# Hybrid encoder trunk: the background row sums of the modulation one batch at a time, loaded a unit ahead, and the first value weights split in the front

## The chip, the cores and the metric

One core of one Trainium2 chip. The metric is the time of one execution in device microseconds (us), as the median of a few runs. PE is the tensor engine (matmuls), DVE the vector engine (VectorE), ACT the scalar engine, POOL GpSimd, SP the engine that issues nearly all DMAs (SyncE).

## The reference

Two batches, a prompt and a sample, of 512 rows and 1024 columns each go through one layer in float32. What matters here:

```python
c_act = jax.nn.silu(c)
mod = c_act @ w_ada[l] + b_ada[l]
sh1, sc1, g1, sh2, sc2, g2 = jnp.split(mod, 6, axis=-1)
h = rms_norm(x, norm1_g[l]) * (1.0 + sc1) + sh1
proj = h @ w_in[l]                       # 768 columns for attention, 4 x 512 for retention
o_a = windowed_attention(...)            # 8 heads, 2 of keys and values, window 128
o_r = bidirectional_retention(...)       # 4 heads, chunks of 128, forward and backward
x = x + g1 * (concat(o_a, o_r) @ w_out[l])
h = rms_norm(x, norm2_g[l]) * (1.0 + sc2) + sh2
x = x + g2 * (square(relu(h @ w_mlp1[l])) @ w_mlp2[l])
```

and a last normalisation. The modulation `mod` has six sections of 1024 numbers for each batch: section 0 is sh1, 1 is sc1, 2 is g1, 3 is sh2, 4 is sc2 and 5 is g2.

## The kernel before

**Products.** A float32 product is made of three matmuls (`mm3`, L122 to L124): each operand is split into a high part, cast by ACT (`split_high`, L93, tiles `wh_...`), and a low part, the difference, made by VectorE (L99, tiles `wl_...`). Weights that both batches need are split once, for batch 0, and both parts are stored in device memory (`kept_...`) and loaded again for batch 1 (`kept_unit`, L117).

**Stages.** The *front* normalises batch 0 and makes the first 768 columns of its projection (`first`, keys, values and queries of attention). It is a list of steps written by hand (`FRONT`), and each engine keeps the order of that list up to the step P.7.0 (`pin`). P.k.c is the part of column block c from the 128 rows k; `keep.k` stores the split weights of k. After the front work goes by *units*, each with one 512 KB weight: load, split, matmuls (`pj_rv`, `pj_rq`, ...). Phase 1 has 16 units for batch 0 (4 of the retention's values, rv, and 12 of its queries, keys and gates, rq, rk, rg). Phase 2 has 22 units for batch 1 (6 of attention, which load what the front kept, 4 rv, 12 others). Phase 3 has the 8 units of batch 0's output projection (`po`, weights `wo`). Then come batch 1's output projection and the feed-forward part, which takes from about 500 us to the end.

**Between the units.** The weight of unit n+1 is loaded while unit n is computed (`run_units`). Each unit has two halves, and behind each half `between` moves the blocks of attention (`psc` scores, `ppt`, `po`) and of retention on by a step: `prs` are the scores of retention, VectorE multiplies them with a decay table (`rsf`, L409), ACT and VectorE split them (`rsc`, L411 and L412), PE makes `py`, ACT copies it (`ryt`, L429), PE transposes it (`pyn`), VectorE takes its mean and variance (`bn`, `mv`, L437 and L438), POOL takes the power (`rrs`), ACT normalises (`ryn`, L447), PE transposes back (`pyb`). `ks` and `qs` are the split keys and queries of attention.

**The background.** What batch 1's first normalisation and the later sections of `mod` need is not made by matmuls but by sums along rows on VectorE: a 128 x 1024 tile of the transposed weights (`raw_adat_...`) times the activations of one batch, summed (L172, `jka_...`, where the product itself goes to a junk tile out of the six buffers of tag `f2`, which `ryt` and others use too). There are 60 such sums on 36 loaded tiles: 12 for batch 1 alone (sections 1 and 0), and 24 tiles of sections 2, 4 and 3 with both batches. `run_units` takes one tick of the background at the end of each unit; a tick issues the load of one tile and right behind it the sums, one or two, of that tile:

```python
    def ada_unit(sec, kc, bs, dst, name, bias=None):
        t = raw_unit(w_ada_t[sec, kc], f"adat_{name}_{sec}_{kc}", sec > 1)
        reduce_unit(t, sec, kc, bs, dst, name, bias)
```

Sections 0 and 1 load into three buffers shared with the weights (tag `raw`), the others into the 32 buffers of tag `r4`. Behind the front a scheduler sets each engine's order: the program gives priorities, and what its own model takes for ready goes first. So neighbouring sums can come to stand together, and a load can stand in SP's queue behind a load that still waits for a buffer.

Of the kernel before, what the change touches and what calls it, by code (L numbers as in the profile page):

```python
# [32 lines left out]
def trunk_kernel(ctx, tc, x0, x1, x0_t, x1_t, params, gate2_bias, w_ada_first, w_ada_t, w_ada_gate2, w_in_first, w_in,  # L33
# [62 lines left out]
    def split_unit(src, name, n):  # L96
        t = raw_unit(src, name)
        w = split_high(t, name)
        nc.vector.tensor_sub(w[1], t, f(w[0]))  # L99
# [69 lines left out]

    def reduce_unit(t, sec, kc, bs, dst, name, bias=None):  # L170
        for b in bs:
            nc.vector.tensor_tensor_reduce(junk(f"jka_{name}_{sec}_{kc}_{b}"), t, cb[:, b, :], 1.0,  # L172
                                           bcol[:, sec * KC + kc:sec * KC + kc + 1] if bias is None else bias,
                                           ALU.mult, ALU.add, dst(b))

    def mod_chunk(which, is_scale, kc, bs):
        sec = which * 3 + (1 if is_scale else 0)
        if is_scale:
            ada_unit(sec, kc, bs, lambda b: mod_a[which][:, kc, b:b + 1], "s", onep[:, which * KC + kc:which * KC + kc + 1])
            for b in bs:  # L180
                a_ = mod_a[which][:, kc, b:b + 1]
                nc.vector.tensor_tensor(a_, a_, gcol[which][:, kc:kc + 1], ALU.mult)
        else:
            ada_unit(sec, kc, bs, lambda b: mod_s[which][:, kc, b:b + 1], "s")

    def first_mods(b):

        for kc in [k for k in range(KC) if k not in BOTH]:
            for s in (1, 0):
                mod_chunk(0, s == 1, kc, (b,))  # L190
                yield

    def ada_columns(which, is_scale):
        for kc in range(KC):
            mod_chunk(which, is_scale, kc, range(NB))
            yield

    def gate_rows(which):

        gm = const.tile([P, NB, KC], F32, name=f"gm_{which}")  # L200
        for kc in range(KC):
            ada_unit(which * 3 + 2, kc, range(NB), lambda b: gm[:, b, kc:kc + 1], "g")
            yield
        pg = aux_bank(f"pgt_{which}")
        nc.tensor.transpose(pg[:NB * KC, :P], gm.rearrange("p b k -> p (b k)"), ident)
        gr_ = mwork.tile([NB * KC, P], F32, tag="st", name=f"gr_{which}", bufs=8)
        nc.scalar.copy(gr_, pg[:NB * KC, :P])
        nc.gpsimd.dma_start(gates[which * NB:(which + 1) * NB, :].rearrange("b (k n) -> (b k) n", n=P), gr_)
        yield
# [1309 lines left out]
```

## Time and profile before

| | |
|---|---|
| median of 3 runs | 1142.35 us (1141.02 to 1143.53) |
| the profiled execution | 1146.14 us, its span 1144.4 us |
| busy in the span: PE, DVE, ACT, POOL | 1095.9, 878.1, 502.3, 40.8 us |
| mean granted clock of PE | 0.986 |
| DMA: moved, mean rate | 232.73 MB, 203 GB/s |

A row of a timeline gives the start, the length, the engine, the line of the kernel, the operation with its output and inputs, and in brackets how long the engine stood idle before it and what released it. Matmul rows overlap, since PE pipelines them: 0.39 us long, they start every 0.23 us.

### The profile page before, as it was taken

The numbers are of one execution on the slowest core, as the hardware profiler recorded it, in microseconds if no ns is written. First come the engines' busy times: TensorE is split into PE (matmuls) and PEld (weight loads), VectorE is DVE, ScalarE is ACT, GpSimd is POOL, SyncE is SP. The second block draws the span as 40 slices with busy tenths as digits, with TensorE's granted clock in tenths as the row PEclk, the third lists the DMA queues.
The fourth block names the chain that finished last, engine by engine and source line by source line (L and its number), as shares of the span: only waits on it lengthen the run. The fifth ranks groups of instructions, "written<-read, shape, count | busy, mean of one in ns | idle before, by whom it ended". The sixth has DMA issues, their size and how long they took to land.

```text
span 1144.4 us, 14016 instructions
## 1 busy us (share of the span) xinstructions
PE 1095.9 (96%) x4997; PEld 893.3 (78%) x4997; DVE 878.1 (77%) x1474; ACT 502.3 (44%) x861; POOL 40.8 (4%) x54
## 2 busy tenths in 40 slices
PE   8989999999899799998999999999999999999996
PEld 5778887777688578887878888888887888888885
DVE  8879888677777656698998787877659854499685
ACT  6565766334552335345433333333344543334341
POOL 1000000000000000100000000000000000001112
PEclk9989999999999979999999999999999999999999
DMA  9976798765455738951655355534693565625503
GB/s 371 361 291 226 246 346 293 224 204 166 147 169 181 271 119 304 352 181 47 214 182 184 138 184 175 185 138 147 199 390 101 166 197 189 221 91 183 179 26 148
DMA packets 86746, 232.73 MB, mean 203 GB/s; under 512 B 8578, under 2 KB 20882, under 8 KB 86676
## 3 DMA queue, kind: packets, MB, share of 16 engines
q1 hardware_dynamic: 86228, 231.51, 58.5%
q8 instruction: 39, 0.64, 0.2%
q10 hardware_dynamic: 288, 0.31, 0.1%
q14 instruction: 31, 0.25, 0.1%
q0 software_dynamic: 160, 0.02, 0.0%
HBM read 160.75 MB, written 71.06 MB: 203 GB/s over the span
## 4 chain that ended last, share of the span: by engine, by line
PE 68%; DVE 16%; DMA 8%; ACT 3%; issue 3%; POOL 1%; SPq 1%; POOLq 0%; DVEq 0%; ACTq 0%
PE px_None L901 12%; PE x L1304 11%; PE y L1304 10%; PE py_None L901 9%; PE po L122 3%; PE po L123 2%; PE po L124 2%; DVE jka_s L172 2%; DMA raw_adat_s<-in_w_ada_t_dram 2%; DMA raw_adat_g<-in_w_ada_t_dram 2%; PE ppt L379 1%; PE po L386 1%; PE psc L353 1%; DMA ur<-spill 1%; DVE jka_f L172 1%
## 5 line engine op out<-in xcount | busy, mean ns | idle before, releaser
L1244 DVE TENSOR_TENSOR uc_l<-ur,uc_h 128x1024 fp32r<-128x1024 f32 x56 | 68.4, 1221 | 53.7 <-ACT uc_h L1244 36.6
L1304 PE MATMUL x<-wc_l,uc_h 128*128 128x512 f32 x256 | 99.8, 390 | 0.8 <-DVE wc_l L1244 0.8
L1304 PE MATMUL x<-wc_h,uc_h 128*128 128x512 f32 x256 | 99.4, 389 | 0.5 <-DVE u L919 0.5
L1304 PE MATMUL x<-wc_h,uc_l 128*128 128x512 f32 x256 | 99.6, 389 | 0.0
L1244 ACT CAST uc_h<-ur 128x1024 fp32r<-128x1024 f32 x56 | 58.8, 1051 | 74.1 <-PE x L1304 30.9
L1304 PE MATMUL y<-wc_h,uc_h 128*128 128x512 f32 x192 | 74.7, 389 | 0.0
L1304 PE MATMUL y<-wc_l,uc_h 128*128 128x512 f32 x192 | 74.7, 389 | 0.0
L1304 PE MATMUL y<-wc_h,uc_l 128*128 128x512 f32 x192 | 74.7, 389 | 0.0
L1244 ACT CAST wc_h<-w 128x1024 fp32r<-128x1024 f32 x48 | 50.4, 1050 | 48.1 <-PE x L1304 23.9
L1244 DVE TENSOR_TENSOR wc_l<-w,wc_h 128x1024 fp32r<-128x1024 f32 x48 | 58.5, 1220 | 13.6 <-ACT wc_h L1244 11.4
L1304 PEld LDWEIGHTS x<-wc_l,uc_h 128*128 128x128 f32 x256 | 48.0, 188 | 11.6 <-DVE wc_l L1244 1.6
L1304 PEld LDWEIGHTS x<-wc_h,uc_h 128*128 128x128 f32 x256 | 48.1, 188 | 10.9 <-issue 0.9
L1304 PEld LDWEIGHTS x<-wc_h,uc_l 128*128 128x128 f32 x256 | 48.1, 188 | 9.8
L122 PE MATMUL po<-wh_wo,ms 128*128 128x512 f32 x128 | 51.8, 405 | 0.0
L124 PE MATMUL po<-wh_wo,ms 128*128 128x512 f32 x128 | 50.9, 398 | 0.0
L123 PE MATMUL po<-wl_wo,ms 128*128 128x512 f32 x128 | 50.8, 397 | 0.0
L806 ACT CAST wc_s4h<-raw_w 128x1024 fp32r<-128x1024 f32 x16 | 16.8, 1052 | 62.2 <-PE px_None L901 36.6
L363 ACT ACTIVATE st<-st,negm 128x256 f32<-128x256 f32 (+1 forms) x64 | 35.2, 555 | 15.5 <-DVE negm L358 15.5
L1304 PEld LDWEIGHTS y<-wc_l,uc_h 128*128 128x128 f32 x192 | 36.0, 188 | 7.5
L1304 PEld LDWEIGHTS y<-wc_h,uc_h 128*128 128x128 f32 x192 | 36.0, 188 | 7.5
L1304 PEld LDWEIGHTS y<-wc_h,uc_l 128*128 128x128 f32 x192 | 36.0, 188 | 7.4
L411 ACT CAST rsc<-rsf 128x512 fp32r<-128x512 f32 x32 | 19.7, 621 | 49.2 <-DVE rsf L409 49.2
(375 smaller groups left out, 3026.7 us busy)
## 6 DMA issues: line engine op xcount, KB each, us to landing
ur<-spill SPq DMA_DIRECT2D x56, 512.0 KB, 4.3
raw_w<-in_w_mlp_dram SPq DMA_DIRECT2D x32, 512.0 KB, 3.5
spill<-s SPq DMA_DIRECT2D x64, 256.0 KB, 3.2
w<-in_w_mlp_dram SPq DMA_DIRECT2D x32, 512.0 KB, 4.5
raw_adat_s<-in_w_ada_t_dram SPq DMA_DIRECT2D x28, 512.0 KB, 6.2
spill<-u SPq DMA_DIRECT2D x48, 256.0 KB, 2.0
raw_ada<-in_w_ada_t_dram SPq DMA_DIRECT2D x12, 512.0 KB, 9.6
x<-in_x_dram SPq DMA_DIRECT2D x12, 512.0 KB, 8.2
```

The source lines that it names most:

```text
L122: nc.tensor.matmul(ps, lhs[0], rhs[0], start=start, stop=False)
L123: nc.tensor.matmul(ps, lhs[0], rhs[1], start=False, stop=False)
L124: nc.tensor.matmul(ps, lhs[1], rhs[0], start=False, stop=stop)
L172: nc.vector.tensor_tensor_reduce(junk(f"jka_{name}_{sec}_{kc}_{b}"), t, cb[:, b, :], 1.0, bcol[:, sec * KC + kc:sec * KC + kc + 1] if bias ...
L353: nc.tensor.matmul(psc[:, :w], qs[hh][:, isl], k_[:, s, j0 * P:j1 * P], start=(s == 0), stop=(s == 1))
L363: nc.scalar.activation(st[hh][:, :w], st[hh][:, :w], AF.Exp, bias=negm[:, hh:hh + 1], scale=0.125, accum_out=den[:, hh:hh + 1])
L379: nc.tensor.transpose(pt[:, hh * P:(hh + 1) * P], st[hh][:, jj * P:(jj + 1) * P], ident)
L411: nc.scalar.copy(sc[sb][:, 0, :], sf)
L806: nc.scalar.copy(hi, src)
L901: self.last = nc.tensor.matmul(bank[:, cs], x[:, k, :], y, start=first and k == 0 and i == 0, stop=last and k == 3 and i == 2, skip_group_ ...
L1244: last_split[:] = [nc.scalar.copy(hi, src), nc.vector.tensor_sub(lo, src, f(hi))]
L1304: nc.tensor.matmul(out, left[n][x][:, i, ts_], right[n][y][:, i, :], start=first and i == 0 and k == 0, stop=end and i == 1 and k == 2, sk ...
```

## The change

**The background.** One generator, `background_mods`, takes the place of `first_mods`, `gate_rows` and `ada_columns`. It goes through the same tiles in the same order (12 for batch 1 alone, then sections 2, 4, 3 with both batches). Each of its steps makes one sum. The load of tile n+1 is issued at the first step of tile n, and all tiles are in the 32 buffers of `r4`. Each sum is issued with `issue_after` on VectorE's last instruction before it in the program, so that the scheduler does not put it ahead of that one. The ticks are no longer taken at the end of a unit but in `between`, 0.7 for each half of a unit, so 1.4 for a unit.

**The front.** The load of the first value weights (`rvl.0`) stands behind `wi.7`, the last load of the front's own weights; their cast (`rvh.0`) and difference (`rvs.0`) ahead of P.7.0, and the load of the second ones behind these. The `keep` steps are spread among the earlier P steps.

```diff
-    def ada_unit(sec, kc, bs, dst, name, bias=None):
-
-        t = raw_unit(w_ada_t[sec, kc], f"adat_{name}_{sec}_{kc}", sec > 1)
-        reduce_unit(t, sec, kc, bs, dst, name, bias)
...
+    def last_of(engine):
+        return next(i for i in reversed(nc.cur_bb.bb.instructions) if i.engine == engine)
+
+    gm = const.tile([P, NB, KC], F32, name="gm")
+
+    def background_mods():
+        todo = [(s, kc, (1,)) for kc in range(KC) if kc not in BOTH for s in (1, 0)]
+        todo += [(s, kc, range(NB)) for s in (2, 4, 3) for kc in range(KC)]
+
+        def load(n):
+            return raw_unit(w_ada_t[todo[n][0], todo[n][1]], f"adat_{n}", True) if n < len(todo) else None
+        nxt = load(0)
+        yield
+        for n, (sec, kc, bs) in enumerate(todo):
+            t, nxt = nxt, load(n + 1)
+            which, is_scale = divmod(sec, 3)
             for b in bs:
...
+                with tc.issue_after(last_of(mybir.EngineType.DVE)):
+                    reduce_unit(t, sec, kc, (b,), lambda _: dst, "b",
+                                onep[:, which * KC + kc:which * KC + kc + 1] if is_scale == 1 else None)
+                    if is_scale == 1:
+                        nc.vector.tensor_tensor(dst, dst, gcol[which][:, kc:kc + 1], ALU.mult)
                 yield
...
+            if sec == 2 and kc == KC - 1:
+                pg = aux_bank("pgt")
...
@@ between @@
+        clock[2] += clock[3]
+        while clock[2] > 0.999:
+            clock[2] -= 1.0
+            tick_background()
         clock[1] = min(clock[1] + rate, 3.0)
...
@@ run_units @@
-    def run_units(units, rate, hooks={}, pace=1.0):
-        due = 0.0
+    def run_units(units, rate, hooks={}, pace=0.7):
+        clock[3] = pace
         nxt = units[0].load()
...
             for _ in u.use(cur):
                 between(rate)
-            due += pace
-            if due > 0.999:
-                due -= 1.0
-                tick_background()
...
@@ ret_v_units, load @@
-                return split_unit(w_in_v[kq], f"rv{b}_{kq}", 512)
+                t = one.pop(("rv", kq), None) or raw_unit(w_in_v[kq], f"rv{b}_{kq}")
+                return split_raw(t, f"rv{b}_{kq}", 512)
...
+    def step_rvs(kq):
+        t, w = one["rv", kq]
+        nc.vector.tensor_sub(w[1], t, f(w[0]))
+        first_v[kq].loaded([x.rearrange("p (a n) -> p a n", n=512) for x in w])
...
@@ FRONT, its last lines @@
-hm.7 hl.6 wl.7 P.6.0 lg.6 P.6.1 lg.7 hl.7 P.6.2 P.6.3 P.6.4 P.6.5 keep.6 P.7.0 P.7.1 P.7.2 P.7.3
-P.7.4 P.7.5 keep.7
+wl.7 P.6.0 keep.4 lg.6 P.6.1 lg.7 hl.7 P.6.2 P.6.3 keep.5 P.6.4 P.6.5 rvh.0 rvs.0 rvl.1 P.7.0 P.7.1
+P.7.2 P.7.3 keep.6 P.7.4 P.7.5 keep.7
...
-    background.extend([first_mods(1), gate_rows(0), ada_columns(1, True), ada_columns(1, False)])
+    background.append(background_mods())
```

On PE at the end of the front, before (`first` is the projection, `pvt_a` a transposition of the values, `psc` the first scores, `pj_rv` the first value unit):

```order
L124 MATMUL first_312<-h_0_7_510,wil_441 128x512
L316 MATMUL pvt_a_635<-ident,vt_a_566 128x128 x4
L353 MATMUL psc_0_0_0_648<-ks_0_553,qs_0_573 128x256 x2
L353 MATMUL psc_0_0_1_652<-ks_0_553,qs_0_573 128x256 x2
L122 MATMUL pj_rv_0_619<-wh_rv_0_606,h_0_0_243 128x512
L122 MATMUL pj_rv_1_620<-wh_rv_0_606,h_0_0_243 128x512
L353 MATMUL psc_0_0_2_656<-ks_0_553,qs_1_581 128x256 x2
L122 MATMUL pj_rv_2_621<-wh_rv_0_606,h_0_0_243 128x512
L123 MATMUL pj_rv_0_619<-wl_rv_0_607,h_0_0_243 128x512
L124 MATMUL pj_rv_0_619<-wh_rv_0_606,h_0_0_243 128x512
```

and now:

```order
L126 MATMUL first_313<-h_0_7_511,wil_446 128x512
L124 MATMUL pj_rv_0_620<-wh_rv_0_551,h_0_0_244 128x512
L125 MATMUL pj_rv_0_620<-wl_rv_0_552,h_0_0_244 128x512
L126 MATMUL pj_rv_0_620<-wh_rv_0_551,h_0_0_244 128x512
L124 MATMUL pj_rv_0_620<-wh_rv_0_551,h_0_1_261 128x512
L125 MATMUL pj_rv_0_620<-wl_rv_0_552,h_0_1_261 128x512
L126 MATMUL pj_rv_0_620<-wh_rv_0_551,h_0_1_261 128x512
L314 MATMUL pvt_a_636<-ident,vt_a_573 128x128 x4
L124 MATMUL pj_rv_1_621<-wh_rv_0_551,h_0_0_244 128x512
L125 MATMUL pj_rv_1_621<-wl_rv_0_552,h_0_0_244 128x512
L126 MATMUL pj_rv_1_621<-wh_rv_0_551,h_0_0_244 128x512
L124 MATMUL pj_rv_1_621<-wh_rv_0_551,h_0_1_261 128x512
```

Matmuls of the first value unit, 12 in these rows, moved ahead of the scores.

On SP early in phase 2, before (the `kept_first` loads are weights of attention for batch 1; `raw_adat_g_3` is the tile of section 2 whose sums are `jka_g_3_0` and `jka_g_3_1`):

```order
L88 DMA raw_adat_g_2_2023<-in_w_ada_t_dram 128x1024
L117 DMA wh_q_0_2197<-kept_first 128x8x128
L117 DMA wl_q_0_2199<-kept_first 128x8x128
L117 DMA wh_q_1_2259<-kept_first 128x8x128
L117 DMA wh_q_2_2342<-kept_first 128x8x128
L88 DMA raw_adat_g_3_2109<-in_w_ada_t_dram 128x1024
L117 DMA wl_q_1_2261<-kept_first 128x8x128
L117 DMA wl_q_2_2344<-kept_first 128x8x128
```

and now (the numbers after `raw_adat` only count tiles; 1988 is the fifth tile of section 2, 2108 the sixth, 2216 the seventh):

```order
L119 DMA wl_v_2127<-kept_first 128x8x128
L88 DMA raw_adat_1988<-in_w_ada_t_dram 128x1024
L119 DMA wl_q_0_2201<-kept_first 128x8x128
L119 DMA wh_q_0_2199<-kept_first 128x8x128
L119 DMA wh_q_1_2261<-kept_first 128x8x128
L88 DMA raw_adat_2108<-in_w_ada_t_dram 128x1024
L523 DMA kept_t_101<-dtab_3_2184 128x896
L119 DMA wh_q_2_2342<-kept_first 128x8x128
L119 DMA wl_q_1_2263<-kept_first 128x8x128
L119 DMA wh_q_3_2412<-kept_first 128x8x128
L119 DMA wl_q_2_2344<-kept_first 128x8x128
L88 DMA raw_adat_2216<-in_w_ada_t_dram 128x1024
```

The tiles stand earlier among the same weights: the one ahead of `wl_q_0` is now the fifth, where the third stood before, and the sixth stands ahead of `wh_q_2`, which the fourth stood behind.

On DVE at the end of phase 2, before (`jka_s_5` and `jka_s_6` are tiles 5 and 6 of section 3; `bn_1` is the retention's second head, `wl_wo` a weight of the output projection):

```order
L291 TENSOR_TENSOR rk_3_3798<-pj_rk_3_3768,rk_3_3798 128x512
L99 TENSOR_TENSOR wl_wo_0_1_3910<-raw_wo_0_1_3907,wh_wo_0_1_3909 128x1024
L172 ISA jka_s_5_0_3713,mod_s_90<-raw_adat_s_5_3711,cb,cols 128x1024
L172 ISA mod_s_90 128x1
L172 ISA jka_s_5_1_3715,mod_s_90<-raw_adat_s_5_3711,cb,cols 128x1024
L172 ISA mod_s_90 128x1
L172 ISA jka_s_6_0_3760,mod_s_90<-raw_adat_s_6_3758,cb,cols 128x1024
L172 ISA mod_s_90 128x1
L172 ISA jka_s_6_1_3762,mod_s_90<-raw_adat_s_6_3758,cb,cols 128x1024
L172 ISA mod_s_90 128x1
L437 BN_STATS bn_1_0_3807<-pyn_1_3801 128x6
```

and now (`jka_b_1` and `jka_b_2` are tiles 1 and 2 of section 3):

```order
L289 TENSOR_TENSOR rq_3_3725<-pj_rq_3_3697,rq_3_3725 128x512
L170 ISA jka_b_1_1_3728,mod_s_90<-raw_adat_3601,cb,cols 128x1024
L170 ISA mod_s_90 128x1
L170 ISA jka_b_2_0_3755,mod_s_90<-raw_adat_3648,cb,cols 128x1024
L170 ISA mod_s_90 128x1
L101 TENSOR_TENSOR wl_wo_0_0_3874<-raw_wo_0_0_3871,wh_wo_0_0_3873 128x1024
L435 BN_STATS bn_1_0_3783<-pyn_1_3777 128x6
L289 TENSOR_TENSOR rk_3_3774<-pj_rk_3_3740,rk_3_3774 128x512
L436 BN_AGGR mv_1_3782<-bn_1_0_3783 128x2
```

Of the four sums ahead of `bn_1` two are left, and they belong to earlier tiles; the sums of tiles 5 and 6 moved into phase 3.

More of the change, by code (lines that the diff above doesn't have):

```diff
@@ L96, in split_unit, with split_raw @@
     def split_unit(src, name, n):
-        t = raw_unit(src, name)
+        return split_raw(raw_unit(src, name), name, n)
+    def split_raw(t, name, n):
         w = split_high(t, name)
@@ L174, in reduce_unit @@
                                            ALU.mult, ALU.add, dst(b))
[L176 to L179, printed above, removed]
-            for b in bs:
[L181 to L190, printed above, removed]
-                yield
[L193 to L209, printed above, removed]
+    def last_of(engine):
+        return next(i for i in reversed(nc.cur_bb.bb.instructions) if i.engine == engine)
@@ new lines, in trunk_kernel @@
+    gm = const.tile([P, NB, KC], F32, name="gm")
[9 more added lines that the diff above has]
+            which, is_scale = divmod(sec, 3)
+            for b in bs:
+                dst = (mod_s[which], mod_a[which], None)[is_scale]
+                dst = gm[:, b, kc:kc + 1] if dst is None else dst[:, kc, b:b + 1]
+                with tc.issue_after(last_of(mybir.EngineType.DVE)):
[3 more added lines that the diff above has]
+                        nc.vector.tensor_tensor(dst, dst, gcol[which][:, kc:kc + 1], ALU.mult)
+                yield
+            if sec == 2 and kc == KC - 1:
+                pg = aux_bank("pgt")
+                nc.tensor.transpose(pg[:NB * KC, :P], gm.rearrange("p b k -> p (b k)"), ident)
+                gr_ = mwork.tile([NB * KC, P], F32, tag="st", name="gr", bufs=8)
+                nc.scalar.copy(gr_, pg[:NB * KC, :P])
+                nc.gpsimd.dma_start(gates[0:NB, :].rearrange("b (k n) -> (b k) n", n=P), gr_)
+                yield
@@ L529, in trunk_kernel @@
     background, stages, active, extra, later = [], [], [], [], []
-    clock = [0, 0.0]
+    clock = [0, 0.0, 0.0, 0.0]
     def tick_background():
@@ L581, in __init__, with loaded @@
             self.load, self.use, self.done, self.keep = load, use, done, keep
-    def run_units(units, rate, hooks={}, pace=1.0):
-        due = 0.0
+        def loaded(self, w):
+            self.load = lambda: w
+    def run_units(units, rate, hooks={}, pace=0.7):
+        clock[3] = pace
         nxt = units[0].load()
@@ L649, in trunk_kernel @@
     ret_v = [[], []]
+    one = {}
     hT_of = [[], []]
@@ L935, in store @@
                 nc.sync.dma_start(spill[g][p, :, i, :], t)
-    wi, halves, sums, mr, hm, banks, open_banks, one = {}, {}, {}, {}, {}, {}, {}, {}
+    wi, halves, sums, mr, hm, banks, open_banks = {}, {}, {}, {}, {}, {}, {}
     order = (4, 5, 0, 1, 2, 3)
@@ L1086, in step_warm, with step_rvl, step_rvh @@
             nc.tensor.transpose(b_[:, :P], ident, ident)
+    def step_rvl(kq):
+        one["rv", kq] = raw_unit(w_in_v[kq], f"rv0_{kq}")
+    def step_rvh(kq):
+        one["rv", kq] = one["rv", kq], split_high(one["rv", kq], f"rv0_{kq}")
+    def step_rvs(kq):
+        t, w = one["rv", kq]
+        nc.vector.tensor_sub(w[1], t, f(w[0]))
+        first_v[kq].loaded([x.rearrange("p (a n) -> p a n", n=512) for x in w])
     logs = log_decays()
-    steps = dict(x=step_x, nat=step_nat, tr=step_tr, wi=step_wi, tanh=step_tanh, cact=step_cact, cbt=step_cbt, cbc=step_cbc,
+    steps = dict(rvl=step_rvl, rvh=step_rvh, rvs=step_rvs, x=step_x, nat=step_nat, tr=step_tr, wi=step_wi, tanh=step_tanh, cact=step_cact, cbt=step_cbt, cbc=step_cbc,
                  sq=step_sq, ad=step_ad, ns=step_ns, nv=step_nv, nr=step_nr, rbt=step_rbt, rbc=step_rbc, xn=step_xn,
@@ L1103, in trunk_kernel @@
 P.1.5 P.2.0 tr.6.0 wl.3 P.2.1 wh.4 hl.3 P.2.2 wi.5 xn.2 P.2.3 tr.7.1 P.2.4 C.5.1 hh.4 P.2.5 hm.4
-tr.7.0 P.3.0 C.5.0 wh.5 P.3.1 wi.6 P.3.2 wl.4 hh.5 wi.7 P.3.3 hm.5 hl.4 P.3.4 C.6.1 P.3.5 wh.6 P.4.0
-C.6.0 P.4.1 wh.7 P.4.2 wl.5 P.4.3 hl.5 P.4.4 xn.3 P.4.5 keep.0 keep.1 keep.2 keep.3 keep.4 P.5.0
-lg.0 C.7.1 hh.6 P.5.1 lg.1 hm.6 P.5.2 lg.2 C.7.0 P.5.3 lg.3 wl.6 P.5.4 lg.4 hh.7 P.5.5 keep.5 lg.5
-hm.7 hl.6 wl.7 P.6.0 lg.6 P.6.1 lg.7 hl.7 P.6.2 P.6.3 P.6.4 P.6.5 keep.6 P.7.0 P.7.1 P.7.2 P.7.3
-P.7.4 P.7.5 keep.7
+tr.7.0 P.3.0 C.5.0 wh.5 P.3.1 wi.6 P.3.2 wl.4 hh.5 wi.7 rvl.0 P.3.3 hm.5 hl.4 P.3.4 C.6.1 P.3.5 wh.6
+P.4.0 keep.0 C.6.0 P.4.1 wh.7 P.4.2 wl.5 P.4.3 keep.1 hl.5 P.4.4 xn.3 P.4.5 P.5.0 keep.2 lg.0 C.7.1
+hh.6 P.5.1 lg.1 hm.6 P.5.2 lg.2 C.7.0 P.5.3 keep.3 lg.3 wl.6 P.5.4 lg.4 hh.7 P.5.5 lg.5 hm.7 hl.6
+wl.7 P.6.0 keep.4 lg.6 P.6.1 lg.7 hl.7 P.6.2 P.6.3 keep.5 P.6.4 P.6.5 rvh.0 rvs.0 rvl.1 P.7.0 P.7.1
+P.7.2 P.7.3 keep.6 P.7.4 P.7.5 keep.7
     """.split()
@@ L1112, in trunk_kernel @@
     first = attn_units(hT_of[0], 0)
+    first_v = ret_v_units(hT_of[0], 0)
     for name in FRONT:
@@ L1149, in norm_x1 @@
             yield
-    background.extend([first_mods(1), gate_rows(0), ada_columns(1, True), ada_columns(1, False)])
-    units = ret_v_units(hT[0], 0)
+    background.append(background_mods())
+    units = first_v
     for h in range(RH):
-        units += ret_units(hT[0], 0, h)
-    run_units(units, 1.3, {7: lambda: extra.append(norm_x1())}, pace=1.0)
+        units = units + ret_units(hT[0], 0, h)
+    run_units(units, 1.3, {7: lambda: extra.append(norm_x1())})
     units = attn_units(hT[1], 1) + ret_v_units(hT[1], 1)
```

## The prediction

> **What bounds the kernel now.** I read the list of engines on the page first, then the run cut into stages at places where PE's picture changes, then PE's chain of waits, then the timelines around the waits. The page says that PE is the bound:
>
> ```profile
> span 1144.4 us, 14016 instructions
> PE 1095.9 (96%) x4997; PEld 893.3 (78%) x4997; DVE 878.1 (77%) x1474; ACT 502.3 (44%) x861; POOL 40.8 (4%) x54
> ```
>
> So 1144.4 - 1095.9 = 48.5 us of PE idle is all that can be won without taking matmuls out, plus what PE loses where its clock is halved. The change takes no matmul out. The stages (columns: window, length, busy us and count for PE, PEld, DVE, ACT, POOL, then granted clock, DMA share, GB/s) say where these 48.5 us lie:
>
> ```profile
> 57.00:68.00 11.00, 6.96 (x19) 5.28 (x20) 10.57 (x19) 6.38 (x11) 0.00 (x0) 0.69 0.57 196
> 68.00:171.00 103.00, 102.98 (x506) 84.44 (x505) 86.56 (x213) 69.03 (x156) 1.99 (x1) 1.00 0.82 285
> 171.00:206.00 35.00, 33.23 (x152) 26.14 (x150) 28.93 (x57) 23.74 (x38) 2.02 (x2) 1.00 0.92 297
> 206.00:292.00 86.00, 76.15 (x341) 59.74 (x342) 62.91 (x154) 31.97 (x75) 2.73 (x3) 0.97 0.59 189
> 345.00:413.00 68.00, 58.16 (x240) 44.98 (x239) 48.47 (x97) 21.29 (x40) 2.01 (x2) 0.90 0.53 183
> 413.00:486.00 73.00, 73.00 (x347) 60.70 (x346) 44.27 (x85) 30.14 (x57) 5.02 (x6) 1.00 0.84 302
> 238.58:241.99 3.41, 1.66 (x7) 0.99 (x8) 2.83 (x10) 1.74 (x5) 1.01 (x1) 1.00 0.83 233
> 241.99:245.40 3.41, 3.41 (x10) 2.73 (x10) 3.38 (x6) 1.79 (x4) 0.00 (x0) 0.50 0.18 74
> ```
>
> Three places are at stake: the handover from the front (57 to 68: 4.0 us idle, clock 0.69), the attention and early retention of batch 1 (206 to 292: 9.9 us) and the end of batch 1's retention (345 to 413: 9.8 us, clock 0.90). Phase 1 (68 to 171) and phase 3 (413 to 486) have PE full, so there the change can only lose.
>
> **What ends these waits.** PE's own rows (start, length, what it waited for):
>
> ```profile
> 56.10 0.60 PE L316 MATMUL pvt_a<-ident,vt_a 128*128 128x128 f32 x4
> 58.92 0.50 PE L353 MATMUL psc<-ks,qs 128*128 128x256 f32 x2 [2.22 <-DVE qs L331]
> 61.54 0.77 PE L353 MATMUL psc<-ks,qs 128*128 128x256 f32 x2 [2.12 <-DVE qs L331]
> 67.61 0.53 PE L123 MATMUL pj_rv<-wl_rv,h 128*128 128x512 f32 x1
> 220.28 0.50 PE L122 MATMUL py<-rsc,rv 128*128 128x512 f32 x1 [0.86 <-ACT rsc L411]
> 228.84 0.50 PE L122 MATMUL py<-rsc,rv 128*128 128x512 f32 x1 [1.42 <-ACT rsc L411]
> 240.14 0.50 PE L122 MATMUL pj_q<-h,wh_q 128*128 128x512 f32 x1 [1.58 <-DVE qs L331]
> 289.56 0.63 PE L122 MATMUL pj_rq<-h,wh_rq 128*128 128x512 f32 x1 [2.79 <-DVE rv L291]
> 393.70 0.66 PE L433 MATMUL pyn<-ident,ryt 128*128 128x128 f32 x4 [2.97 <-ACT ryt L429]
> 399.98 1.52 PE L452 MATMUL pyb<-ident,ryn 128*128 128x128 f32 x4 [4.23 <-ACT ryn L447]
> 406.55 0.80 PE L122 MATMUL py<-rsc,rv 128*128 128x512 f32 x1 [2.09 <-ACT rsc L411]
> ```
>
> The producers named (rsc, qs, ryn) are short. What makes them late stands ahead of them on VectorE: a pair of row sums, and ahead of the pair a load that has not landed. VectorE's waits from 50 to 460 us, its timeline at two of these places, and SyncE's queue, which issued that load late:
>
> ```profile
> DVE jka_s L172 <- DMA raw_adat_s<-in_w_ada_t_dram: 12.3, 6, 4.3
> DVE jka_g L172 <- DMA raw_adat_g<-in_w_ada_t_dram: 11.4, 5, 3.5
> 199.25 10.45 SPq L117 DMA_DIRECT2D wh_q<-kept_first  x2
> 209.75 0.65 SPq L88 DMA_DIRECT2D raw_adat_g<-in_w_ada_t_dram  x1
> 214.94 1.28 DVE L172 CUSTOM_DVE_ANT_0 jka_g<-raw_adat_g,cb,cols 128x1024 bf16<-128x1024 f32 x1 [2.66 <-DMA raw_adat_g<-in_w_ada_t_dram]
> 225.04 1.29 DVE L172 CUSTOM_DVE_ANT_0 jka_g<-raw_adat_g,cb,cols 128x1024 bf16<-128x1024 f32 x1 [3.49 <-DMA raw_adat_g<-in_w_ada_t_dram]
> 391.69 1.28 DVE L172 CUSTOM_DVE_ANT_0 jka_s<-raw_adat_s,cb,cols 128x1024 bf16<-128x1024 f32 x1
> 396.51 0.29 DVE L437 BATCH_NORM_STATS2 bn<-pyn 128x6 f32<-128x128 f32 x1
> ```
>
> At 225.04 VectorE stands still for 3.49 us, then sums twice, and only then makes the rsf and rsc that PE takes at 228.84. At 391.69 nothing is late, but four sums in a row take 391.69 to 396.51 = 4.82 us (1.205 each), and the normalisation on which PE's 4.23 us wait hangs begins behind them. Together the seven waits listed from 220 on are 0.86 + 1.42 + 1.58 + 2.79 + 2.97 + 4.23 + 2.09 = 15.9 us.
>
> **The background, step by step.** The number of loads, of row sums and their reading stays. Three things change. (1) One sum per tick, so at most one or two stand together: 1.2 us ahead of a producer in place of 2.4 or 4.8. (2) The load goes out when the unit before it starts. Until now the latency stood openly in VectorE's queue, 12.3 + 11.4 = 23.7 us in 11 waits; with two ticks of lead, and a tick every 0.7 of a unit, the load has 13.4 us (phase 2 is 206 to 413 us for 22 units, 9.4 us each, with 1.4 ticks a unit, so a tick lasts 6.7 us) where SyncE's row shows 5.2 us from issue at 209.75 to use at 214.94. (3) It can still be held in SyncE's queue behind a load that waits for a buffer, as at 199.25; in the changed order the same kept loads of q stand there, one sum later, so I leave part of the first wait standing.
>
> What I take for the seven waits: 0.86 to 0.3, 1.42 to 0.5, 1.58 to 0.6, 2.79 to 0.4 (no four sums ahead of rv), 2.97 to 0 (ryt needs no buffer that a row of sums holds), 4.23 to 1.0 (a POOL power and a copy are left), 2.09 to 0.9. That leaves 3.7, and 15.9 - 3.7 = 12.2 us go. The other small waits of 200 to 412 I leave as they are.
>
> The clock comes on top. From 241.99 to 245.40 it is 0.50 after a stretch in which PE was busy 1.66 us of 3.41, though its longest wait there was 1.58 us. Each such stretch costs 3.41 / 2 = 1.7 us. The window 345 to 413 at clock 0.90 loses 0.10 * 58.16 = 5.8 us of its busy time (I count 5.3, three stretches with the wait at 406.55 taken out), and before it there are two single stretches, at 241.99 and from 289.56 on, where the first row is 0.63 and not 0.40 long: 3.4 us. Of these 8.7 us I take 5.3 as won, and leave two stretches, since waits of 0.5 to 1 us stay. The Trainium skill, "TensorE: Matmul & The Clock Gate", Part 1, in "HAM oscillation", puts the limit at idle gaps over some 3.4 us. The trace disagrees here, since 1.58 us within a half-idle stretch was enough; by the page the two stretches would also go, and the sum would be larger by 3.4 us.
>
> In phase 3 the sums come new: some 10 now stand there (46 units, 0.7 a half: 64 ticks for 62 of them), 10 * 1.2 = 12 us on a VectorE that has 73.00 - 44.27 = 28.7 us free, and 5 loads of 0.5 MB on queues at 0.84. PE never waits there now. The last sums feed the second normalisation at the phase's end, which the order puts behind them as before. I cost it at 0 with an upper bound of 5 * 0.5 MB / 302 GB/s = 8.7 us if no transfer were hidden. Phase 1 gets one or two loads more at a DMA share of 0.82 to 0.92: 0 by cover of PE's full queue, bounded by 2 * 0.5 MB / 297 GB/s = 3.5 us. For new waits from sums that may no longer be moved aside I take 1.5 us off (one sum, 1.2, once or twice exposed); the ends are 0 and 62 * 1.2 = 74, which needs every sum on PE's path and is far from rows in which PE is 96% busy.
>
> Background: 12.2 + 5.3 - 1.5 = 16.0 us.
>
> **The front, step by step.** VectorE's chain ks, qs is what PE waits for twice, while the first value weights are split only behind it:
>
> ```profile
> 51.53 2.06 SPq L88 DMA_DIRECT2D raw_rv<-in_w_in_v_dram  x2
> 60.86 1.99 ACT L93 CAST wh_rv<-raw_rv 128x1024 fp32r<-128x1024 f32 x2
> 56.76 0.69 DVE L303 TENSOR_TENSOR ks<-first,ks 64x512 fp32r<-64x512 f32 x1 [1.27 <-ACT ks L302]
> 58.19 4.54 DVE L331 TENSOR_TENSOR qs<-first,qs 64x512 fp32r<-64x512 f32 x7
> 62.75 2.36 DVE L99 TENSOR_TENSOR wl_rv<-raw_rv,wh_rv 128x1024 fp32r<-128x1024 f32 x2
> 65.05 0.63 PE L122 MATMUL pj_rv<-wh_rv,h 128*128 128x512 f32 x1
> 65.48 0.63 PE L123 MATMUL pj_rv<-wl_rv,h 128*128 128x512 f32 x1
> 229.43 0.40 PE L122 MATMUL pj_q<-h,wh_q 128*128 128x512 f32 x1
> 229.66 0.41 PE L123 MATMUL py<-rsc,rv 128*128 128x512 f32 x1
> ```
>
> Now the load goes out ahead of the 16 stores of keep, cast and difference ahead of the last step, and 18 of unit 0's 24 matmuls stand between the last of kc 7 and the fourth pair of psc. A 512-column matmul starts every 229.66 - 229.43 = 0.23 us at full clock and every 65.48 - 65.05 = 0.43 us at half. 18 * 0.23 = 4.1 us of work for the 2.22 + 2.12 = 4.3 us of wait. From 61.54 to 67.9 PE runs at half clock, which costs another 3.2 us. At stake: 7.5. Against it: the cast (1.0) and the difference (1.2) now stand ahead of the ks and qs chain. VectorE has 1.27 us idle at 56.76 that cover it if the difference falls there, else qs comes 1.2 us later. One half-clock stretch (1.7) may stay. I take 7.5 - 0.8 - 1.7 = 5.0, between 0 (the difference late, the same wait under another name) and 7.5.
>
> **Sum.** 16.0 + 5.0 = 21.0 us. The profiled execution took 1146.1 us (span 1144.4 and 1.7 around it), 3.8 above the median of 1142.35. 1146.1 - 21.0 = 1125.1 for it; against the median 1121.4, called 1122, since an execution 3.8 us quicker may have a little less idle to give.
>
> **Rivals.** A: only part comes. New producers (the power on POOL, 1.0 us a head, ACT's casts) take the places of the sums, half-clock stretches stay: the 5.0 of the front and a third of the 16: 1142.35 - 10 = 1132, between 1127 and 1140. For it: 7 of the listed waits name ACT and DVE, not the load itself. Chance 0.22.
>
> B: all goes: 15.9 + 8.7 + 7.5 = 32 us, 1110. [...] Chance 0.07.
>
> C: slower. Loads in the spare buffers wait for a buffer that PE frees, and in SyncE's queue the weights stand behind them; a sum in fixed order then holds VectorE for it. Its place is 160 to 210 us, where a weight is already late:
>
> ```profile
> 160.72 11.08 DMA raw_rq<-in_w_in_dram
> ```
>
> That load took 11.08 us, where the DMA share goes from 0.82 to 0.92. If loads ahead lengthen each of the 12 weight loads of retention by 3.5 us beyond its lead (two of these rows wait 2.7 and 3.5 on VectorE), the loss is 42 and the time 1163; it decides from 21 / 12 = 1.75 us a load on. The Trainium skill, "DMA: Bandwidth & Descriptors", "Issuing engines are not separate DMA queues", has all transfers interleave on the same 16 engines, which speaks for C: an early load takes its bandwidth from a weight. The trace agrees as far as that one load goes (11.08 us); at the share of 0.59 of 206 to 292 it shows 5.2 us. Chance 0.08.
>
> D: no change. The sums move, but the chain rsf, rsc, ryn was late for itself, and the front's wait goes to the next one: 1142, chance 0.06.
>
> The forecast has 0.57. Two runs of this kernel differ by 1143.53 - 1141.02 = 2.5 us, so 0.2% (2.3 us) is about what can be told from no change. Faster: 0.57 + 0.22 + 0.07 = 0.86, less 0.01 for A's upper edge. The likeliest case alone is 1115 to 1128; the range goes from B's 1110 to 1138, within A's upper part, and leaves C and D out.
>
> **What would show it.** Right: 57 to 68 at 9 us busy or more with pj_rv ahead of the first psc; no wait of VectorE for raw_adat over 1 us; at most two sums in a row; the windows 206 to 292 and 345 to 413 shorter by 6 and 9 us, clock 0.97 and more; phase 3 still full. Wrong: waits of PE in 68 to 206 or in phase 3, VectorE waiting for raw_adat with rsf behind it, or wl_rv ahead of qs with psc at 61 us as before.

## The result and the profile after

The changed kernel takes 1115.07 us (median of 5 runs, 1113.65 to 1116.22), the kernel before 1142.35 (1141.02 to 1143.53): 27.3 us less, a ratio of 0.976 with a 95% interval of 0.9746 to 0.9775. The forecast was 1122, with a range of 1110 to 1138. The head of the page and the stages that the prediction cut (same windows and columns):

```profile
span 1113.7 us, 14016 instructions
PE 1081.6 (97%) x4997; PEld 886.7 (80%) x4997; DVE 878.2 (79%) x1474; ACT 502.6 (45%) x861; POOL 39.4 (4%) x54
...
57.00:68.00 11.00, 9.10 (x44) 7.02 (x43) 10.02 (x22) 6.17 (x13) 0.00 (x0) 1.00 1.03 390
68.00:171.00 103.00, 99.60 (x484) 82.01 (x482) 89.48 (x215) 68.15 (x154) 1.02 (x1) 0.98 0.83 300
171.00:206.00 35.00, 33.12 (x151) 25.94 (x150) 27.95 (x56) 23.64 (x38) 2.85 (x2) 1.00 0.79 254
206.00:292.00 86.00, 85.20 (x417) 69.61 (x416) 69.88 (x181) 42.46 (x106) 2.74 (x3) 1.00 0.58 189
345.00:413.00 68.00, 66.72 (x302) 54.06 (x301) 49.39 (x98) 26.03 (x47) 3.02 (x3) 1.00 0.73 259
413.00:486.00 73.00, 71.87 (x353) 59.55 (x352) 59.52 (x109) 32.13 (x68) 3.10 (x6) 1.00 0.77 282
```

VectorE and ACT do the same work as before (878.2 and 502.6 us). PE is busy for 1081.6 and not 1095.9 us, with the same number of matmuls: most of the 14.3 us are stretches at half clock that are gone (the mean clock rose from 0.986 to 0.996, about 11 us of the span). Its idle time fell from 48.5 to 32.1 us. The two stages that had 9.9 and 9.8 us idle have 0.8 and 1.3, at clock 1.00. What is new stands in phase 1, which was full before and now has 3.4 us idle and a clock of 0.98. PE's waits from 45 to 460 us of 0.7 us and more are now these:

```profile
47.29 0.50 PE L125 MATMUL first<-h,wih 128*128 128x512 f32 x1 [1.10 <-DVE h L284]
58.15 0.47 PE L124 MATMUL pj_rv<-wh_rv,h 128*128 128x512 f32 x1 [0.82 <-DVE ks L302]
60.78 0.47 PE L124 MATMUL pj_rv<-wh_rv,h 128*128 128x512 f32 x1 [0.77 <-DVE qs L329]
91.19 0.50 PE L124 MATMUL pj_rq<-h,wh_rq 128*128 128x512 f32 x1 [0.81 <-DVE rv L289]
135.47 0.80 PE L126 MATMUL pj_rg<-h,wl_rg 128*128 128x512 f32 x1 [2.51 <-DVE wl_rg L101]
184.93 0.33 PE L450 MATMUL pyb<-ident,ryn 128*128 128x128 f32 x1 [0.80 <-ACT ryn L445]
252.90 0.66 PE L377 MATMUL ppt<-ident,st 128*128 128x128 f32 x4 [0.72 <-DVE mx L353]
377.04 0.51 PE L124 MATMUL py<-rsc,rv 128*128 128x512 f32 x1 [1.01 <-ACT rsc L409]
```

Following the same matmul in both traces gives the account by stage. The first `pj_rq` (end of the first value units) starts at 91.19 and not 96.00, 4.8 us earlier. The first `pj_k` (start of phase 2) starts at 195.61 and not 196.99: of the 4.8 only 1.4 are left, so phase 1 lost 3.4. The first `po` of the output projection starts at 377.56 and not 407.14, 29.6 earlier, and the first `px` (transpositions of `x`) at 441.07 and not 471.34, 30.3 earlier. Phase 2 alone gave 28.2 us. (The profiled execution of before was 3.8 us above its median and that of the changed kernel 0.4, which is about what lies between 30.3 here and 27.3 in the medians.) Phase 2, from its first `pj_k` to the first `po`, holds 865 and 864 of PE's instructions, before and now:

```profile
196.99:407.14 210.15, 189.03 (x865) 149.59 (x863) 155.97 (x382) 85.35 (x198) 5.75 (x6) 0.96 0.59 191
195.61:377.56 181.95, 179.65 (x864) 147.03 (x862) 139.87 (x352) 87.66 (x201) 5.76 (x6) 1.00 0.59 196
```

So PE's idle time in it fell from 21.1 to 2.3 us, which is 18.8 of the 28.2, and its busy time by 9.4 us, as the clock rose from 0.96 to 1.00.

### The profile page after: what moved, and what is told of

Same layout as the page of the kernel before. It is cut to its first block, busy times and chain, and to the rows that moved or that the text cites. A ratio compares the mean times of both kernels' runs of the same rounds, so it can differ in the third digit from the quotient of the medians.

```text
span 1113.7 us, 14016 instructions
## 1 busy us (share of the span) xinstructions
PE 1081.6 (97%) x4997; PEld 886.7 (80%) x4997; DVE 878.2 (79%) x1474; ACT 502.6 (45%) x861; POOL 39.4 (4%) x54
## 4 chain that ended last, share of the span: by engine, by line
PE 72%; DVE 17%; ACT 4%; DMA 3%; issue 3%; POOL 1%; POOLq 0%; DVEq 0%; ACTq 0%
PE px_None L904 13%; PE x L1319 13%; PE py_None L904 10%; PE y L1319 10%; PE po L124 2%; DVE jka_b L170 2%; PE po L125 2%; PE po L126 2%; PE po L384 2%; PE ppt L377 2%; PE psc L351 1%; PE pj_rq L124 1%; PE pj_rq L126 1%; PE pj_rq L125 1%; DVE jka_f L170 1%
## 5 line engine op out<-in xcount | busy, mean ns | idle before, releaser
L124 PE MATMUL po<-wh_wo,ms 128*128 128x512 f32 x128 | 50.9, 397 | 0.9 <-DMA wh_wo<-kept_wo 0.6
L126 PE MATMUL po<-wh_wo,ms 128*128 128x512 f32 x128 | 49.4, 390 | 0.0
L170 DVE CUSTOM_DVE_ANT_0 jka_b<-raw_adat,cb,cols 128x1024 bf16<-128x1024 f32 x38 | 48.2, 1279 | 0.1
```

The lines of the kernel that those rows point to most:

```text
L124: nc.tensor.matmul(ps, lhs[0], rhs[0], start=start, stop=False)
L126: nc.tensor.matmul(ps, lhs[1], rhs[0], start=False, stop=stop)
```

## The experiments

Each run stands against executions of the kernel before on the same chip; times are medians, ratios have 95% intervals. The runs were made in three groups of four, in the order below, each on another chip; the kernel before took 1142.45, 1142.79 and 1143.19 us there. Between groups the ratios compare better than the times.

**The front alone.** The kernel before, with the steps rvl, rvh, rvs and the spread keep steps; the background untouched.

```diff
-hm.7 hl.6 wl.7 P.6.0 lg.6 P.6.1 lg.7 hl.7 P.6.2 P.6.3 P.6.4 P.6.5 keep.6 P.7.0 P.7.1 P.7.2 P.7.3
+wl.7 P.6.0 keep.4 lg.6 P.6.1 lg.7 hl.7 P.6.2 P.6.3 keep.5 P.6.4 P.6.5 rvh.0 rvs.0 rvl.1 P.7.0 P.7.1
...
```

> The kernel before with the front's part alone (first value weights loaded, cast and subtracted in the front, keep steps spread); the background is that of before. Theory: the first rq matmul of phase 1 came 4.8 us earlier in the changed kernel (96.0 to 91.19), and that is the front's own; here it comes earlier by 4 to 6 us, PE stays full to 171 us, and the time is 1136 to 1139. Rival: phase 1 is held by its loads (share 0.82 to 0.92), so that a handover 5 us earlier only waits there: in the changed kernel phase 2 began only 1.4 us earlier (196.99 to 195.61). Then 1140 to 1142.

1137.36 us, ratio 0.9949 (0.9934 to 0.9963). The first `pj_rq` stands at 90.84 and the first `pj_k` at 191.37, 5.6 us earlier than before; nothing was lost in phase 1. So the front's part is worth 5.1 us, and the rival, that phase 1 is held by its loads, falls.

**The background alone.** The changed kernel with the old front list.

> The changed kernel with the front's list of before: the background alone. Theory (the parts add): 1115.1 + 4.8 = 1119 to 1121. Rival: the front's gain is eaten by phase 1's waits in the changed kernel (3.4 us lost between 91 and 196), so that the background alone gives 1115 to 1117.

1116.97 us, ratio 0.9773 (0.9756 to 0.979). That is 25.5 us by itself. With the front's 5.1 it would be 30.6, and both together gave 27.3: the parts do not add, 3.3 us are missing. Here the rival was right. The 2.51 us wait at 135 us is 0.92 in this run (`pj_rg` at 137.48), and the clock of 68 to 171 is 1.00.

**Only the load a unit ahead.** The kernel before, its tick and its pairs, with the generator of the change that loads ahead:

```diff
+        nxt = load(0)
+        for n, (sec, kc, bs) in enumerate(todo):
+            t, nxt = nxt, load(n + 1)
+            for b in bs:                # both sums, in one tick at the unit's end, no issue_after
```

> The kernel before with one thing changed: the tile of the background is loaded a unit ahead, into the 32 buffers; both sums still stand in one tick at the end of a unit, and their order is left to the scheduler. Theory (late loads and sums in groups both matter): VectorE's 23.7 us of waits for raw_adat go, pairs and fours of sums stay; 1129 to 1135, with the wait ahead of the last heads (393 to 407 us) still there. Rival 1 (the late load is all): 1117 to 1122. Rival 2 (the grouping is all): 1139 to 1143.

1113.22 us, ratio 0.9747 (0.973 to 0.9764): 29.2 us, more than the whole background of the change. The first rival, that the late load is all (1117 to 1122), came nearest, and the gain is larger still; my theory had 1129 to 1135. VectorE waits 1.2 us for the tiles, in place of 23.7:

```profile
DVE jka_b L172 <- DMA raw_adat<-in_w_ada_t_dram: 1.2, 2, 1.1
```

VectorE's timeline still shows 11 pairs, but no group of four: with the loads issued earlier the scheduler places the sums otherwise. So this run takes away the late loads and the group of four at once.

**One sum per tick, in order, without the lead.** The changed kernel with the load issued in the tick of its first sum.

```diff
-            t, nxt = nxt, load(n + 1)
+            t = load(n)
```

> The changed kernel with the load issued in the tick of its first sum, not a unit ahead; one sum per tick, in order, as changed. Theory (both matter, and a sum kept in order makes a late load worse): VectorE waits for raw_adat again, at up to 36 tiles by 3 to 5 us each, less what PE's queue covers; 1125 to 1135. Rival 1 (the late load is all): 1137 or more, perhaps slower than before. Rival 2 (the grouping is all): 1114 to 1118.

1134.48 us, ratio 0.9924 (0.9907 to 0.9941). Of the 8.0 us won 5.1 are the front's, so one sum at a time, in order, spread into phase 3, gives some 3 us without the lead, if the two parts add. VectorE waits for tiles again, and PE for what is queued behind them (the waits views for VectorE, 50 to 460 us, and PE):

```profile
DVE jka_b L170 <- DMA raw_adat<-in_w_ada_t_dram: 19.0, 9, 4.9
...
PE py L124 <- ACT rsc L408: 9.2, 6, 4.6
```

The time lies at the slow end of what the theory gave and short of the first rival's 1137.

**Pairs ahead and the front.** The third run with the changed front.

> The kernel before with the tile loaded a unit ahead (both sums in one tick at the unit's end, not kept in order) and the changed front: the changed kernel without one sum per tick, without the fixed order and without the ticks spread into phase 3. Theory now (the late load was all of the background's gain; one sum at a time in order brings nothing, and in phase 1 costs the 2.5 us wait at 135 us and the half clock behind it): 1113.2 - 5.1 = 1107 to 1110, with PE full from 64 to 171 us. Rival (the two parts do not add, because phase 1 loses whatever the front wins, as in the changed kernel): 1112 to 1115.

1109.23 us, ratio 0.97 (0.9683 to 0.9716): 4.0 us below pairs ahead alone, near the front's 5.1. PE has 102.85 of 103 us busy from 68 to 171, and the range of the theory holds the time:

```profile
68.00:171.00 103.00, 102.85 (x504) 83.74 (x503) 89.99 (x216) 72.82 (x163) 1.02 (x1) 1.00 0.80 287
206.00:292.00 86.00, 85.25 (x413) 69.27 (x412) 73.73 (x191) 40.74 (x102) 2.74 (x3) 1.00 0.63 208
345.00:413.00 68.00, 67.88 (x310) 55.51 (x309) 47.68 (x95) 27.13 (x51) 3.02 (x3) 1.00 0.74 260
```

**Only the buffers.** The kernel before with the first 12 tiles in the 32 buffers, no lead (`True` in place of `sec > 1` in `ada_unit`).

> The kernel before with the first 12 tiles of the background in the 32 buffers instead of the three that the weights use; load and sums in one tick as before. Theory (the lead is what counts): VectorE still waits for the tiles of sections 2 to 3, so 1139 to 1143. Rival (loading ahead worked by freeing the weights' three buffers): 1112 to 1125.

1146.97 us, ratio 1.0028 (1.0012 to 1.0044). The other buffers give nothing and cost some 3 us; this is a little above the range that I gave. So the gain of the run with pairs does not come from the buffers.

**Four sums together, with the lead.** Two tiles at every second unit, loaded two ahead.

```diff
-            t, nxt = nxt, load(n + 1)
+            if n % 2 == 0:
+                cur, nxt = nxt, [load(n + 2), load(n + 3)]
+            t = cur[n % 2]
...
+            if n % 2 == 1:
+                yield
                 yield
```

> Loads ahead as in the run with pairs, but two tiles at every second unit, so that up to four sums stand together (in VectorE's order now two groups of four and five of three, before one of four). Theory (sums that have their data cost PE nothing, since PE has other work queued): 1112 to 1117. Rival (a row of sums delays what stands behind it, as my prediction had it for the waits of 2.97 and 4.23 us at 393 to 400 us): 1118 to 1128, with PE waiting for ryn, rsc or qs behind a group of three or four.

1115.61 us, ratio 0.976 (0.9745 to 0.9776), as the theory had it: 2.4 us above the run with pairs, which was made on another chip and whose ratio, 0.9747 (0.973 to 0.9764), is not clearly different. Two groups of four and five of three now stand in VectorE's timeline. The one at 178.73 shows on PE: behind it `wl_rk` is made, for which PE waits 1.26 us (VectorE's rows, the sums between left out, and PE's):

```profile
178.73 1.28 DVE L172 CUSTOM_DVE_ANT_0 jka_b<-raw_adat,cb,cols 128x1024 bf16<-128x1024 f32 x1
...
183.55 1.22 DVE L99 TENSOR_TENSOR wl_rk<-raw_rk,wh_rk 128x1024 fp32r<-128x1024 f32 x1
...
184.82 0.55 PE L124 MATMUL pj_rk<-h,wl_rk 128*128 128x512 f32 x1 [1.26 <-DVE wl_rk L99]
```

So seven groups of three and four that have their data cost 2.4 us in all, or nothing that can be told from noise. The loads also go out earlier here than with pairs, so the run does not vary the groups alone.

**The changed kernel without the fixed place.** `with tc.issue_after(...)` taken out; the rest as changed.

> The changed kernel without the fixed place of each sum in VectorE's queue (the scheduler may put it elsewhere); one sum per tick, loads a unit ahead, ticks spread, front as changed. Theory (the fixed place costs the wait at 135 us): 1108 to 1112. Rival (the fixed place is needed, since the scheduler moves sums up ahead of what PE waits for): 1117 to 1125. Third: no difference, 1114 to 1116.

1108.08 us, ratio 0.9691 (0.9675 to 0.9706): 7.0 us below the changed kernel, the theory's time. Its reason was only partly right: the wait for `wl_rg` is still there, 1.83 and not 2.51 us.

```profile
133.98 0.50 PE L126 MATMUL pj_rg<-h,wl_rg 128*128 128x512 f32 x1 [1.83 <-DVE wl_rg L101]
```

By the same matmuls in both traces, 1.6 of the 7 us are won up to the third `pj_rq` (146.62 and 145.07), 1.7 more up to phase 2 (195.61 and 192.31), nothing much in phase 2 up to its last gate (367.61 and 364.26), and 2.8 from there to `po` (377.56 and 371.44). So the fixed place seems to cost a little at several places; of the last 2.8 us a part is only moved, since 32 of PE's instructions stand in that stretch and not 39.

**Another queue for the loads.** The kernel before with the tiles issued from POOL's queue and not SyncE's; load and sums in one tick.

```diff
-        nc.sync.dma_start(t, w_ada_t[sec, kc])
+        nc.gpsimd.dma_start(t, w_ada_t[sec, kc])
```

> The kernel before with one thing changed: the background's tiles are issued from POOL's queue instead of SyncE's, so that they do not stand behind weights that wait for a buffer; load and sums in one tick as before. It tells why the load was late. Theory (mostly its place in SyncE's queue, as at 199.25 to 209.75 us): VectorE's waits for the tiles fall from 23.7 us to under 12, and the time is 1118 to 1132. Rival (mostly the 4 to 8 us from issue to landing, which no queue shortens): 1138 to 1144. Below both: POOL itself, whose power stands behind a load that waits for a buffer, becomes a new wait: above 1144.

1132.74 us, ratio 0.9908 (0.9889 to 0.9926), just above the theory's range. Its first half holds: out of SyncE's queue the waits for tiles fall from 23.7 to 1.9 us. The tick of the program is the same, but on the chip the loads now have a lead. By the rows of issue and of the first sum of each tile, the 18 loads issued between 195 and 365 us go out 8.7 to 27.9 us ahead of their sum, in the median 18.0; before it was 5.2 to 12.1, in the median 7.2. From issue to landing they take 4.3 us in the median, before 5.8. So most of the lateness was the place in SyncE's queue, behind weights that waited for a buffer. And the waits before 292 go (206 to 292: PE busy 83.60 of 86). But the end of phase 2 stays as it was: the group of four sums is there, and behind it PE waits as before. There the loads are late again, since on POOL they stand behind a power (`rrs`) that waits for VectorE: the tiles summed at 376.95 and 389.70 go out 6.4 and 4.1 us ahead of that, and these are the 1.9 us of waits that are left (waits view; POOL's, VectorE's and PE's timeline; a window):

```profile
DVE jka_s L173 <- DMA raw_adat_s<-in_w_ada_t_dram: 1.9, 2, 1.4
...
369.59 1.03 POOL L443 TENSOR_TENSOR rrs<-rva,neghalf 128x4 f32<-128x4 f32 x1 [22.92 <-DVE rva L441]
370.60 1.12 POOL L168 DMA_DIRECT2D raw_adat_s<-in_w_ada_t_dram  x2
...
376.95 1.28 DVE L173 CUSTOM_DVE_ANT_0 jka_s<-raw_adat_s,cb,cols 128x1024 bf16<-128x1024 f32 x1 [1.43 <-DMA raw_adat_s<-in_w_ada_t_dram]
...
382.91 0.29 DVE L438 BATCH_NORM_STATS2 bn<-pyn 128x6 f32<-128x128 f32 x1
...
378.97 1.12 PE L434 MATMUL pyn<-ident,ryt 128*128 128x128 f32 x4 [2.56 <-ACT ryt L430]
386.41 1.52 PE L453 MATMUL pyb<-ident,ryn 128*128 128x128 f32 x4 [3.88 <-ACT ryn L448]
393.51 0.80 PE L122 MATMUL py<-rsc,rv 128*128 128x512 f32 x1 [2.61 <-ACT rsc L412]
...
345.00:413.00 68.00, 58.60 (x235) 45.65 (x234) 44.70 (x84) 21.49 (x39) 4.25 (x6) 0.87 0.51 175
```

From the last gate unit to `po` it takes 25.0 us (369.07 to 394.11), before 23.6, with pairs ahead 8.9 (368.52 to 377.39). These stretches do not hold the same work (54, 54 and 39 of PE's instructions), but PE is idle in them for 9.4, 9.5 and 0.1 us. The run parts the loss of before into two: the late loads ahead of this end, some 10 us, and the end itself.

**Half a unit of lead.** As with pairs ahead, but the load goes out after the unit's first half.

> The kernel before with the tile loaded half a unit ahead (issued after the unit's first half, summed at its end), pairs left to the scheduler. A unit lasts about 9 us in phase 2, so the lead is some 4.5 us, against 3.3 to 8.2 us from issue to landing. Theory (the lead has to cover issue to landing): part of the gain of the run with a whole unit (29 us), 1120 to 1132. Rival (any lead is enough): 1112 to 1117.

1123.65 us, ratio 0.9832 (0.9807 to 0.9857), within the theory: 19.5 of the 29.2 us. VectorE still waits for tiles, in 9 places:

```profile
DVE jka_b L172 <- DMA raw_adat<-in_w_ada_t_dram: 14.2, 9, 3.7
...
206.00:292.00 86.00, 78.60 (x367) 62.69 (x367) 69.36 (x170) 36.75 (x87) 2.73 (x3) 0.98 0.59 195
345.00:413.00 68.00, 67.47 (x305) 54.59 (x305) 51.03 (x102) 26.09 (x48) 3.02 (x3) 1.00 0.64 219
```

Here it is the other way round than in POOL's queue: the end is cured (no group of four), the stage from 206 to 292 is not. The lead in the program is not the lead on the chip: of the loads issued between 195 and 365 us the median goes out 8.2 us ahead of its sum here, 7.2 before and 9.7 with pairs ahead, while VectorE's waits for them are 8.4, 19.3 and 1.3 us.

**Pairs, ahead, front, and the fixed place.**

> The run with pairs a unit ahead and the changed front (1109.2), with one thing added: each sum is kept behind VectorE's last instruction before it in the program. Theory (the fixed place costs by itself, as the 7.0 us between the changed kernel and the same without it say): 1114 to 1120. Rival (it costs only together with one sum per tick, where twice as many places in the queue are fixed): 1108 to 1111.

1112.81 us, ratio 0.9733 (0.9715 to 0.9751), against 1109.23 without the fixed place: 3.6 us, between the two ranges. The fixed place costs by itself, and more with one sum per tick (7.0), where the 60 sums stand in 60 places and not in 36; that the number of places is the reason is not shown.

**A faster background.** The changed kernel at pace 1.0 for each half unit, so two sums a unit.

> The changed kernel with the pace 1.0 a half unit instead of 0.7: two sums a unit, one per tick and in order, so that no sums are left for phase 3. Theory (the pace does not matter, the fixed place costs some 7 us at either): 1113 to 1118. Rival (spreading into phase 3 is worth something, because VectorE is busier in phase 2): 1118 to 1125. Third (the ticks in phase 3 cost): 1108 to 1112.

1127.8 us, ratio 0.9866 (0.9848 to 0.9885). I had it at 1113 to 1118; it is 12.7 us slower than at 0.7 and slower than every rival said. Phase 1 now has 26 sums (19 at 0.7), and PE waits in it for low parts of weights:

```profile
68.00:171.00 103.00, 97.96 (x473) 79.38 (x472) 92.91 (x225) 67.16 (x152) 1.99 (x1) 0.98 0.84 304
206.00:292.00 86.00, 79.88 (x366) 63.30 (x365) 68.59 (x174) 36.94 (x83) 3.04 (x3) 0.98 0.60 200
```

Most of the 12.7 us is lost later, though. Against the changed kernel phase 2 begins 1.6 us later (`pj_k` at 197.25), its last gate unit 15.6 us (383.25) and `po` 12.4 us (389.96). Pairs a unit ahead have 42 sums in phase 2, more than the 34 here, and no such loss, so it is not the rate alone. Pairs, ahead, front and the fixed place have 44 sums there in a fixed place, and no such loss either, so it is not the rate together with the fixed place. One sum at each half unit is left, but no run had that without the fixed place, and the cause stays open.

## Why the prediction was right, and where it was not

**The front: right in mechanism and size.** 5.0 us were forecast, 4.8 stand in the trace and 5.1 in the run of the front alone. The two waits of 2.22 and 2.12 us became 0.82 and 0.77 (and 0.31 for `wl_rv`), and 57 to 68 is at full clock, so the half-clock stretch that I left standing went. That the sum came out is in part luck: these three waits are 1.9 us where I took off 0.8, which the prediction works out from no row, and the 1.7 us taken off for the clock were not needed.

**The late loads: right, and the cause named is shown.** Step (2) had them as the cause; a load a unit ahead gives 29.2 us by itself. Its lead of 13.4 us against 5.2 us is in the trace 17.6 against 5.8 (medians of the loads issued from 195 to 365 us). Step (3), SyncE's queue, is shown by the run in POOL's queue: 23.7 us of VectorE's waits become 1.9. The size was wrong. I had sized what remains of the seven waits too carefully. Of 15.9 us I left 3.7; at the places that answer to them stands only the 1.01 at 377.04 (the 0.72 at 252.90 was not among the seven). The other waits, which I left as they are, went too; three of them were not small (1.05, 1.67 and 1.11 us at 258.69, 276.56 and 314.25). And no stretch of phase 2 is left at half clock, where I left 3.4 us: the two windows are at 1.00. Phase 2 gave 28.2, the forecast for the background 16.0 (17.5 without its new waits): 18.8 us of idle time for the 12.2 forecast, and 9.4 us by the clock for 5.3. Against that phase 1 lost 3.4 us, which I had at nothing (with 1.5 us for new waits wherever they come), and the two errors partly cancel in the time. Rival B, that all goes, is nearer to what phase 2 shows than my forecast; in the time, 1110, it is 5 us off and mine 7.

**The page on the clock.** I had kept the two stretches because in the trace of before PE's longest wait in one window (238.58 to 241.99) was 1.58 us and yet the clock fell, against the rule of the Trainium skill, "TensorE: Matmul & The Clock Gate", Part 1, "HAM oscillation", that idle gaps over some 3.4 us do that. I had also taken it that waits of 0.5 to 1 us would keep two such stretches. No trace of this case shows that: between 40 and 500 us every half-clock stretch begins behind a window of 3.41 us in which PE is busy at most 2.16 us and waits once for 1.18 us or more (both at 286.63 in the run at pace 1.0). The sum that I gave for the page, 3.4 us more, came nearer; not because gaps of that size are harmless, but because the gaps went. The new wait at 135.47 says so, 2.51 us long in a window in which PE is busy 0.89 of 3.40 us, followed by half clock:

```profile
132.60:136.00 3.40, 0.89 (x3) 0.50 (x2) 3.33 (x7) 3.01 (x9) 0.00 (x0) 0.89 0.00 0
136.00:138.00 2.00, 2.00 (x7) 1.46 (x6) 1.62 (x3) 0.92 (x2) 0.00 (x0) 0.50 0.89 344
```

**One sum at a time, in order: the step that failed.** Step (1) took the order as a gain, and the new waits as 1.5 us. The runs say: with the lead given, pairs cost nothing that shows (1109.2 against 1108.1 for one sum per tick without the fixed place), groups of three and four cost 2.4 us, which is within the noise, and the fixed place costs 7.0 us (3.6 with pairs). What I had seen at 391.69, four sums ahead of the normalisation, goes with a real cost: all four traces that have this group there (before, the front alone, only the buffers, POOL's queue) take 23.5 to 25 us from the last gate unit to `po`, the others 7 to 13 us. That stretch holds 53 or 54 of PE's instructions in the four and 32 to 48 in the others, so the lengths do not compare as they are; but PE is idle in it for 7.9 to 9.5 us in the four and for at most 2.6 us in the others. It takes no order to dissolve the group; with loads ahead the scheduler does it. A late load alone does not make this end slow: before, no tile is late at the group, and with half a unit of lead VectorE waits 2.67 us for a tile at 362.74 and the end is quick. That the group makes it slow is argued from these traces and VectorE's rows; no run takes away the group alone.

**Phase 1: costed at 0, it lost 3.4 us.** The bound, 3.5, was put on loads; the front alone (PE full) and pairs ahead with the front (102.85 of 103) show that it is not the loads. The wait at 135 us came with one sum per tick and the lead: it is 2.51 us, 0.92 with the old front, 1.83 without the fixed place and 2.18 at pace 1.0. VectorE's rows show one sum ahead of `wl_rg`, behind a `mix` that waited for ACT:

```profile
131.34 0.42 DVE L392 TENSOR_TENSOR mix<-po,otmp 64x256 f32<-64x256 f32 x1 [1.31 <-ACT otmp L387]
...
133.00 1.27 DVE L170 CUSTOM_DVE_ANT_0 jka_b<-raw_adat,cb,cols 128x1024 bf16<-128x1024 f32 x1
...
134.20 1.22 DVE L101 TENSOR_TENSOR wl_rg<-raw_rg,wh_rg 128x1024 fp32r<-128x1024 f32 x1
```

Rival C, a loss in phase 1, was right in its sign there, but had it at 160 to 210 us and through loads.

**Phase 3: right.** VectorE takes 9 sums there, and PE stays busy (window 380 to 456):

```profile
380.00:456.00 76.00, 75.10 (x351) 61.39 (x350) 58.49 (x110) 30.71 (x58) 4.11 (x6) 1.00 0.88 322
```
